# First FFN feature blocks in pieces of 384 and 128 tokens instead of 256 and 256, with another order of all instructions

## The chip, the cores and the metric

The kernel runs on one core of a Trainium2 chip. The metric is the device time of one execution in microseconds (us), lower is better. The median of several runs is given, and beside it one profiled execution, from which all views of the trace come. The engines are TensorE (PE, its weight loads shown apart as PEld), VectorE (DVE), ScalarE (ACT) and GpSimd (POOL); SyncE (SP) issues the transfers.

## The reference

One layer of a hybrid backbone: 512 latent tokens that are also given 256 context tokens, width 1024. Three token mixers (gated linear attention, an S5 state space, grouped-query attention) read one input projection and are merged by gates. What the change touches is the FFN behind them, of 2816 gated features with a convolution of width 3 over the tokens:

```python
def dwconv3(x, w, b):
    xp = jnp.pad(x, ((0, 0), (1, 1), (0, 0)))
    return xp[:, :-2] * w[0] + xp[:, 1:-1] * w[1] + xp[:, 2:] * w[2] + b

def conv_ffn(h, lp):
    u = dwconv3(h @ lp["ffn_up"], lp["ffn_conv_w"], lp["ffn_conv_b"])
    a, v = jnp.split(u, 2, axis=-1)
    return (jax.nn.silu(a) * v) @ lp["ffn_down"]
...
        m_lat = jnp.split((jax.nn.silu(c) @ ada_w[i] + ada_b[i])[:, None, :], 6, axis=-1)
        h_lat = modulate(rms_norm(x, norm_mix_pre[i]), m_lat[0], m_lat[1])
        y_ctx, y_lat = token_mixer(h_ctx, h_lat, lp, rope, not last)
        x = x + m_lat[2] * rms_norm(y_lat, norm_mix_post[i])
        h_lat = modulate(rms_norm(x, norm_ffn_pre[i]), m_lat[3], m_lat[4])
        x = x + m_lat[5] * rms_norm(conv_ffn(h_lat, lp), norm_ffn_post[i])
```

## The kernel before

Each large product is made of three matmuls in fp32r (`mm3`): every operand is split into a high and a low half, and high x high, low x high and high x low are summed in PSUM. So `wuph` and `wupl` are the high and low half of a block of up weights `wup`, `h2h` and `h2l` those of the normalised FFN input. A matmul holds a 128x128 tile of weights, which it loads itself (a PEld record), and streams the tokens through as columns.

The FFN runs over 22 feature blocks of 128 (`NF`), each with two parts, `up{i}0` for the gate and `up{i}1` for the value. A part loads its weights (D), makes the high copy and the low difference, sums 8 slices of the width in one PSUM bank of 512 tokens, and ends with an affine on ScalarE and two convolution steps on VectorE. For blocks 2 to 21 a part has 24 matmuls of 512 columns. For the first two blocks (`NHALF = 2`) the tokens are taken in two pieces, so that each of four parts has 48 matmuls: the first piece can begin before the last tokens are ready. Tokens come ready 128 at a time: `res{t}` adds the mixer's result to the residual for token tile t = 0 to 3, and `h2{t}{n}` scales one half of the width into `tmp`, transposes it with four matmuls into `h2T`, modulates it into `y`, and splits that into `h2h` and `h2l`. The matmuls of the mixer's output projection and of the down projection `ffn_down` write tiles named `tk`, the gate projections `bg`, and the S5 state space has `pT`, `Z`, `win`, `x`, `y5`.

Nothing is ordered by the order of the code. Every instruction is recorded first, and a table `PLACE` gives for each part a letter for each of its instructions (P TensorE, V VectorE, A ScalarE, G GpSimd, D transfer) and a rank; each engine then issues its instructions by rank, and tile buffers are allotted in that order. All instructions are issued by one helper, so the profile has one line, L1223, for nearly all of them, and groups are told apart by tile names.

The loop of the up projection before the change:

```python
            nh = 2 if i < NHALF else 1
            w_ = TL // nh
            for hf in range(nh):
                sl = slice(hf * w_, hf * w_ + w_)
                for k in range(KT):
                    mm3(b[:, sl], wh[:, k * P:k * P + P], wl[:, k * P:k * P + P], h2h[k][:, sl], h2l[k][:, sl],
                        k == 0 and hf == 0, k == KT - 1 and hf == nh - 1, skip_group_check=True)
```

Of the kernel before, what the change touches and what calls it, by code (L numbers as in the profile page):

```python
# [2662 lines left out]
```

## Time and profile before

| | |
|---|---|
| median of 3 runs | 912.75 us (912.71 to 914.13) |
| profiled execution | 912.98 us |
| its span | 910.8 us |
| TensorE busy | 876.1 us, 96% of the span, 4800 matmuls |
| VectorE busy | 612.6 us, 67%, 1118 instructions |
| ScalarE busy | 372.2 us, 41%, 728 |
| GpSimd busy | 230.7 us, 25%, 155 |

The span is what the profile shows; the device time has some 2 us around it. A busy share is an average over stages: the mixer runs to about 531 us, the FFN from there to the end, and each has to be read by itself.

### The profile page before, as it was taken

Reading aid. Unit: us, or ns where it says so; the run is one execution under the profiler, and the core shown is the slowest. Engines: PE = TensorE matmul, PEld = TensorE weight load, DVE = VectorE, ACT = ScalarE, POOL = GpSimd, SP = SyncE. Lnnn points to the kernel's source line nnn. Section 1 sums busy time; section 2 is a strip of 40 time slices with the busy share of each in tenths; the row PEclk is TensorE's granted clock in tenths of the full one; section 3 lists DMA queues with packets and bytes.
Section 4 is the critical chain, followed back from the end, with each engine's and each line's share of the span. In section 5 each row is a group of like instructions: output and inputs, shape, how many; then the busy total and the mean of one; then the engine's idle time right before and its main releaser. Section 6 shows DMA issues by size and latency. Waiting matters only on the chain. (4 is left out here: it accounts for less than half of the span.)

```text
span 910.8 us, 12672 instructions
## 1 busy us (share of the span) xinstructions
PE 876.1 (96%) x4800; PEld 710.8 (78%) x4800; DVE 612.6 (67%) x1118; ACT 372.2 (41%) x728; POOL 230.7 (25%) x155
## 2 busy tenths in 40 slices
PE   6999999989999999999999989999999999999996
PEld 5587867666678888887787868988888888878885
DVE  6988699898985434388967793554556657964223
ACT  3455457567686522044643472233222223420111
POOL 1032002223532333655264133201111023052200
PEclk9999999999999999999999989999999999999999
DMA  9922352230312221437767002221332333432201
GB/s 349 402 81 70 105 150 98 80 133 1 125 47 70 70 93 47 173 108 289 267 220 242 1 1 93 93 93 53 109 116 93 107 103 108 169 116 93 69 24 70
DMA packets 39644, 107.69 MB, mean 118 GB/s; under 512 B 7214, under 2 KB 10942, under 8 KB 39584
## 3 DMA queue, kind: packets, MB, share of 16 engines
q1 hardware_dynamic: 39584, 106.88, 34.1%
q8 instruction: 38, 0.62, 0.3%
q14 instruction: 22, 0.18, 0.1%
HBM read 103.49 MB, written 3.38 MB: 117 GB/s over the span
## 5 line engine op out<-in xcount | busy, mean ns | idle before, releaser
L1223 PE MATMUL up<-h2h,wuph 128*128 128x512 f32 (+1 forms) x384 | 134.4, 374 | 0.5 <-DVE h2h L1223 0.3
L1223 PE MATMUL up<-h2l,wuph 128*128 128x512 f32 (+1 forms) x384 | 134.1, 373 | 0.0
L1223 PE MATMUL up<-h2h,wupl 128*128 128x512 f32 (+1 forms) x384 | 133.6, 372 | 0.0
L1223 DVE SCALAR_TENSOR_TENSOR u<-up,col,u 128x511 f32<-128x511 f32 x88 | 64.6, 746 | 41.0 <-ACT u L1223 39.9
L1223 POOL TENSOR_TENSOR wupl<-wup,wuph 128x1024 fp32r<-128x1024 f32 x15 | 36.9, 2463 | 184.4 <-PE up L1223 93.0
L1223 PEld LDWEIGHTS up<-h2h,wuph 128*128 128x128 f32 x384 | 71.8, 189 | 14.2 <-DVE h2h L1223 0.7
L1223 ACT ACTIVATE u<-up,col 128x512 f32<-128x512 f32 x44 | 33.9, 778 | 118.9 <-PE up L1223 115.0
L1223 PEld LDWEIGHTS up<-h2l,wuph 128*128 128x128 f32 x384 | 72.2, 188 | 13.0
L1223 PEld LDWEIGHTS up<-h2h,wupl 128*128 128x128 f32 x384 | 71.7, 188 | 12.7
L1223 PE MATMUL bg<-hh,wbgl 128*128 128x512 f32 x192 | 75.5, 399 | 1.1 <-DVE wbgl L1223 0.9
L1223 PE MATMUL bg<-hl,wbgh 128*128 128x512 f32 x192 | 75.6, 399 | 0.0
L1223 PE MATMUL bg<-hh,wbgh 128*128 128x512 f32 x192 | 75.2, 398 | 0.0
L1223 DVE TENSOR_TENSOR wupl<-wup,wuph 128x1024 fp32r<-128x1024 f32 x29 | 36.1, 1246 | 45.7 <-PE up L1223 31.1
L1223 PE MATMUL tk<-wtkh,gl 128*128 128x512 f32 x176 | 64.5, 390 | 0.7 <-DVE gl L1223 0.7
L1223 PE MATMUL tk<-wtkh,gh 128*128 128x512 f32 x176 | 64.7, 389 | 0.0
L1223 PE MATMUL tk<-wtkl,gh 128*128 128x512 f32 x176 | 64.6, 389 | 0.0
L1223 POOL TENSOR_TENSOR j<-ada,cbc 128x1024 f32<-128x1024 f32 x16 | 39.9, 2494 | 37.3 <-ACT jb L1223 8.1
L1223 PEld LDWEIGHTS bg<-hh,wbgl 128*128 128x128 f32 x192 | 36.1, 188 | 11.0 <-DVE wbgl L1223 2.0
L1223 PEld LDWEIGHTS bg<-hl,wbgh 128*128 128x128 f32 x192 | 36.1, 188 | 8.9 <-issue 2.0
L1223 PEld LDWEIGHTS bg<-hh,wbgh 128*128 128x128 f32 x192 | 35.9, 188 | 7.7 <-issue 1.0
L1223 PEld LDWEIGHTS tk<-wtkh,gl 128*128 128x128 f32 x176 | 33.0, 188 | 7.9 <-DVE gl L1223 1.1
L1223 POOL TENSOR_TENSOR wbgl<-wbg,wbgh 128x1024 fp32r<-128x1024 f32 x6 | 18.5, 3084 | 81.2 <-DVE wbgh L1223 45.0
(491 smaller groups left out, 2045.9 us busy)
## 6 DMA issues: line engine op xcount, KB each, us to landing
ada<-in_ada SPq DMA_DIRECT2D x48, 512.0 KB
wup<-in_wup SPq DMA_DIRECT2D x44, 512.0 KB
wbg<-in_wbg SPq DMA_DIRECT2D x24, 512.0 KB
wtk<-in_wdn SPq DMA_DIRECT2D x22, 512.0 KB
wP<-in_wP SPq DMA_DIRECT2D x16, 512.0 KB
wbr<-in_wbr SPq DMA_DIRECT2D x8, 512.0 KB
wo<-in_wout SPq DMA_DIRECT2D x16, 256.0 KB
w<-in_wB SPq DMA_DIRECT2D x8, 384.0 KB
```

What stands on the lines that cost most here:

```text
L1223: r = getattr(self.real[e], m)(*a, **k)
```

## The change

The token pieces of the first two feature blocks become 384 and 128 instead of 256 and 256 columns. The number of matmuls stays, 48 for each of four parts; 96 have 384 columns and 96 have 128.

```diff
-            nh = 2 if i < NHALF else 1
-            w_ = TL // nh
+            parts_ = ((0, 3 * P), (3 * P, TL)) if i < NHALF else ((0, TL),)
+            nh = len(parts_)
             for hf in range(nh):
-                sl = slice(hf * w_, hf * w_ + w_)
+                sl = slice(*parts_[hf])
...
-    "up201": ("DAGPPPPPPPPPPPPPPPPPPPPPPPPAVV",
+    "up201": ("DVGPPPPPPPPPPPPPPPPPPPPPPPPAVV",
...
```

The table `PLACE` has new ranks for nearly every instruction, and some letters change: VectorE has as many letters as before (1102), ScalarE 609 instead of 614, GpSimd 156 instead of 151. Of the low halves `wupl`, GpSimd makes 19 instead of 15 and VectorE 25 instead of 29. The following rows show the order at three places.

First, TensorE's queue at the entry to the FFN, before the change. `h2T_1120` and `h2T_1123` are the transposes of token tile 2, `h2T_1134` and `h2T_1137` those of tile 3, `up_1147` is a part of the first blocks, `up_1246` and `up_1356` are whole blocks:

```order
L1223 MATMUL h2T_1120_1193<-cst_1_68,tmp_1119_1192 128x128 x3
L1223 MATMUL up_1147_1220<-h2h_1075_1148,wuph_1145_1218 128x256
L1223 MATMUL h2T_1120_1193<-cst_1_68,tmp_1119_1192 128x128
L1223 MATMUL up_1147_1220<-h2l_1079_1152,wuph_1145_1218 128x256
L1223 MATMUL h2T_1123_1196<-cst_1_68,tmp_1122_1195 128x128 x4
L1223 MATMUL h2T_1134_1207<-cst_1_68,tmp_1133_1206 128x128 x4
L1223 MATMUL h2T_1137_1210<-cst_1_68,tmp_1136_1209 128x128 x4
L1223 MATMUL up_1246_1319<-h2h_1075_1148,wuph_1244_1317 128x512
L1223 MATMUL up_1356_1429<-h2h_1075_1148,wuph_1354_1427 128x512
```

And at the same place after the change:

```order
L1223 MATMUL h2T_1120_1193<-cst_1_68,tmp_1119_1192 128x128 x4
L1223 MATMUL h2T_1123_1196<-cst_1_68,tmp_1122_1195 128x128 x4
L1223 MATMUL h2T_1109_1182<-cst_1_68,tmp_1108_1181 128x128
L1223 MATMUL h2T_1134_1207<-cst_1_68,tmp_1133_1206 128x128 x4
L1223 MATMUL up_1147_1220<-h2h_1075_1148,wuph_1145_1218 128x384
L1223 MATMUL up_1147_1220<-h2l_1079_1152,wuph_1145_1218 128x384
L1223 MATMUL h2T_1137_1210<-cst_1_68,tmp_1136_1209 128x128 x4
L1223 MATMUL up_1246_1319<-h2h_1075_1148,wuph_1244_1317 128x512
L1223 MATMUL up_1356_1429<-h2h_1075_1148,wuph_1354_1427 128x512
```

The two first matmuls of `up_1147` are 384 columns wide and stand behind the transposes of `h2T_1134`, no longer among those of `h2T_1120`; the whole blocks follow at the same row.

Second, TensorE's queue where the second piece of the part `up_1142` begins, after the change (before it, the same part has 256-column rows):

```order
L1223 MATMUL up_1142_1215<-h2h_1078_1151,wupl_1141_1214 128x384
L1223 MATMUL up_1142_1215<-h2h_1078_1151,wuph_1140_1213 128x384
L1223 MATMUL up_1142_1215<-h2l_1082_1155,wuph_1140_1213 128x384
L1223 MATMUL up_1142_1215<-h2h_1078_1151,wupl_1141_1214 128x384
L1223 MATMUL up_1142_1215<-h2h_1075_1148,wuph_1140_1213 128x128
L1223 MATMUL up_1142_1215<-h2l_1079_1152,wuph_1140_1213 128x128
L1223 MATMUL up_1142_1215<-h2h_1075_1148,wupl_1141_1214 128x128
L1223 MATMUL up_1142_1215<-h2h_1075_1148,wuph_1140_1213 128x128
L1223 MATMUL up_1142_1215<-h2l_1079_1152,wuph_1140_1213 128x128
```

From the fifth of these rows on the 128-column matmuls of one part stand one behind another: all 24 lie within 28 rows.

Third, TensorE's queue in the S5 stretch, before the change. `bg` are gate matmuls, `y5_340` reads the states `x__334` and `x__337`:

```order
L1223 MATMUL bg_624_696<-hh_103_170,wbgl_623_695 128x512
L1223 MATMUL bg_624_696<-hh_109_176,wbgh_622_694 128x512
L1223 MATMUL bg_624_696<-hl_110_177,wbgh_622_694 128x512
L1223 MATMUL uT_358_430<-cst_1_68,ug1_357_429 128x96 x2
L1223 MATMUL y5_340_412<-r1_306_378,x__334_406 64x128 x4
L1223 MATMUL y5_340_412<-i1_308_380,x__337_409 64x128 x2
L1223 MATMUL bg_624_696<-hh_109_176,wbgl_623_695 128x512
L1223 MATMUL y5_340_412<-i1_308_380,x__337_409 64x128 x2
```

After the change:

```order
L1223 MATMUL bg_624_696<-hh_98_165,wbgh_622_694 128x512
L1223 MATMUL y5_340_412<-r1_306_378,x__334_406 64x128 x4
L1223 MATMUL bg_624_696<-hl_99_166,wbgh_622_694 128x512
L1223 MATMUL bg_624_696<-hh_98_165,wbgl_623_695 128x512
L1223 MATMUL bg_624_696<-hh_103_170,wbgh_622_694 128x512
L1223 MATMUL bg_624_696<-hl_104_171,wbgh_622_694 128x512
L1223 MATMUL bg_624_696<-hh_103_170,wbgl_623_695 128x512
L1223 MATMUL bg_624_696<-hh_109_176,wbgh_622_694 128x512
L1223 MATMUL y5_340_412<-i1_308_380,x__337_409 64x128 x4
```

Six `bg` matmuls now stand between the two halves of `y5_340`, where none stood. Over the stretch from the last `Z_326` to the first `win_353` there are 63 `bg` matmuls in place of 55.

## Rows read from the trace of the kernel before

**Rows 1.** The page: engine totals, and the chain that ended last by line

```profile
PE 876.1 (96%) x4800; PEld 710.8 (78%) x4800; DVE 612.6 (67%) x1118; ACT 372.2 (41%) x728; POOL 230.7 (25%) x155
...
PE up L1223 26%; PE tk L1223 16%; DMA wup<-in_wup 0%; DVE tmp L1223 0%; PE h2T L1223 0%; DVE ml L1223 0%; POOL wtkl L1223 0%; DVE gl L1223 0%; DVE y L1223 0%; DVE wtkl L1223 0%; DVE wupl L1223 0%; DVE rsy L1223 0%; ACT wuph L1223 0%; DVE rsx L1223 0%; DVE x L1223 0%
```

**Rows 2.** Windows of 20 us at the entry to the FFN and in it

```profile
core 0: us, PE busy (x) PEld busy (x) DVE busy (x) ACT busy (x) POOL busy (x), PEclk, DMA share, GB/s
520.00:540.00 20.00, 16.32 (x81) 13.62 (x80) 17.91 (x69) 15.94 (x49) 2.68 (x4) 0.88 0.00 1
540.00:560.00 20.00, 19.70 (x108) 16.89 (x107) 10.05 (x23) 6.75 (x15) 10.55 (x9) 0.95 0.22 77
560.00:580.00 20.00, 20.00 (x112) 17.47 (x111) 7.24 (x9) 5.01 (x6) 4.91 (x3) 1.00 0.17 56
800.00:820.00 20.00, 19.27 (x86) 15.63 (x85) 15.35 (x15) 6.83 (x9) 12.61 (x8) 1.00 0.38 132
```

**Rows 3.** TensorE's groups, `up`: shape, count, busy us, mean ns, idle us before

```profile
L1223 PE MATMUL up<-h2h,wuph 128*128 128x512 f32 x320 | 117.6, 392 | 0.5 <-DVE h2h L1223 0.3 <-ACT wuph L1223 0.2
L1223 PE MATMUL up<-h2h,wupl 128*128 128x512 f32 x320 | 117.3, 390 | 0.0
...
L1223 PE MATMUL up<-h2h,wuph 128*128 128x256 f32 x64 | 18.4, 287 | 0.0
```

**Rows 4.** Timeline (start us, length us, ...): first and last of 18 gate matmuls

```profile
192.26 0.39 PE L1223 MATMUL bg<-hl,wbgh 128*128 128x512 f32 x1
...
196.13 0.39 PE L1223 MATMUL bg<-hh,wbgh 128*128 128x512 f32 x1
```

**Rows 5.** Timeline of TensorE, first and last of 17 matmuls of 256 columns

```profile
555.00 0.28 PE L1223 MATMUL up<-h2h,wuph 128*128 128x256 f32 x1
...
556.92 0.28 PE L1223 MATMUL up<-h2l,wuph 128*128 128x256 f32 x1
```

**Rows 6.** Weight loads by line and shape, with 128, 32 and 8 columns

```profile
L1223 PEld LDWEIGHTS up<-h2h,wupl 128*128 128x128 f32 x384 | 71.7, 188 | 12.7
...
L1223 PEld LDWEIGHTS ada<-ada,cpad 128*32 128x32 f32 x128 | 3.6, 112 | 4.1 <-issue 1.2 <-DVE cpad L1223 1.0 <-DMA cT<-in_cT 0.4
...
L1223 PEld LDWEIGHTS row<-cst,acc 128*8 128x8 f32 x2 | 0.2, 86 | 0.0
```

**Rows 7.** Timeline, four matmuls of 2 columns and their loads

```profile
21.06 0.52 PEld L1223 LDWEIGHTS ada<-cst,adar 128*128 128x128 f32 x4 [1.50 <-ACT adar L1223]
21.06 0.61 PE L1223 MATMUL ada<-cst,adar 128*128 128x2 f32 x4 [1.02 <-ACT adar L1223]
```

**Rows 8.** Waits of TensorE: total us, times, longest

```profile
PE h2T L1223 <- DVE tmp L1223: 3.7, 1, 3.7
...
PE y L1223 <- DVE x__337_409 L1223: 1.4, 1, 1.4
```

**Rows 9.** Timeline of TensorE at the entry to the FFN

```profile
536.08 0.90 PE L1223 MATMUL h2T<-cst,tmp 128*128 128x128 f32 x3 [3.68 <-DVE tmp L1223]
536.88 0.58 PE L1223 MATMUL up<-h2h,wuph 128*128 128x256 f32 x1
...
537.43 0.55 PE L1223 MATMUL up<-h2l,wuph 128*128 128x256 f32 x1
```

**Rows 10.** Windows of the S5 stretch, a later one, and one in the entry

```profile
170.00:180.00 10.00, 8.46 (x46) 6.70 (x44) 9.91 (x17) 2.86 (x5) 0.00 (x0) 1.00 0.10 26
180.00:190.00 10.00, 6.32 (x57) 3.84 (x59) 9.89 (x14) 7.06 (x21) 5.91 (x2) 1.00 0.00 0
240.00:260.00 20.00, 18.05 (x122) 13.16 (x121) 19.26 (x52) 16.32 (x47) 11.48 (x15) 1.00 0.08 30
...
536.00:537.00 1.00, 0.92 (x4) 0.62 (x4) 1.00 (x6) 1.00 (x4) 0.00 (x0) 0.50 0.03 8
```

**Rows 11.** Groups by line: `wupl` on GpSimd and on VectorE

```profile
L1223 POOL TENSOR_TENSOR wupl<-wup,wuph 128x1024 fp32r<-128x1024 f32 x15 | 36.9, 2463 | 184.4 <-PE up L1223 93.0 <-ACT wuph L1223 26.5 <-DVE u L1223 23.9
...
L1223 DVE TENSOR_TENSOR wupl<-wup,wuph 128x1024 fp32r<-128x1024 f32 x29 | 36.1, 1246 | 45.7 <-PE up L1223 31.1 <-ACT wuph L1223 9.6 <-POOL wupl L1223 4.2
```

More of the change, by code (lines that the diff above doesn't have):

```diff
@@ L285 @@
+        1717, 1720, 1721, 1724]),
+    "rope2": ("VVVVVVAVPPPPVAVAVPPPPA",
+        [1109, 1519, 1672, 1665, 1677, 1680, 1682, 1688, 1711, 1713, 1714, 1722, 1727, 1709, 1715, 1687, 1700, 1723,
+        1725, 1726, 1729, 1733]),
+    "rope3": ("VVVVVVAVPPPPVAVAVPPPPV",
+        [970, 1432, 1603, 1611, 1623, 1633, 1636, 1649, 1654, 1655, 1656, 1658, 1735, 1638, 1652, 1641, 1663, 1659,
+        1660, 1661, 1667, 1738]),
     "ropec0": ("VGAVAVPPPPAA",
-        [1110, 1545, 1564, 1584, 1568, 1588, 1570, 1592, 1607, 1608, 1612, 1621]),
+        [1107, 1353, 1563, 1581, 1571, 1588, 1573, 1583, 1585, 1593, 1598, 1605]),
@@ L303 @@
-    "ap010": ("AAVVGVPPPPAAAVVVGPPPPAPPPPA",
-        [2033, 2043, 2053, 2055, 2060, 2071, 2074, 2076, 2077, 2087, 2095, 2026, 2056, 2073, 2080, 2084, 2093, 2091,
-        2092, 2094, 2096, 2105, 2089, 2090, 2103, 2106, 2111]),
+        [1894, 1900, 1891, 1892, 1977, 1980, 1893, 1896, 1908, 1932, 1992, 2019, 2021]),
+    "ap010": ("AAVVGVPPPPAAAVVGGPPPPAPPPPA",
+        [2030, 2042, 2052, 2055, 2062, 2058, 2069, 2070, 2085, 2088, 2091, 2025, 2053, 2066, 2067, 2071, 2079, 2093,
+        2094, 2097, 2099, 2103, 2089, 2090, 2101, 2105, 2110]),
@@ L306 @@
     "at011": ("PPPPPPPPVVVVV",
[L307 to L310 removed]
+        [1898, 1913, 1866, 1871, 1889, 1915, 1880, 1881, 1916, 1926, 1936, 1942, 1945]),
+    "ap011": ("AAVVGGPPPPAAAVVVGPPPPAPPPPV",
+        [1949, 1955, 1963, 1976, 1985, 1993, 2040, 2041, 2043, 2044, 2048, 1959, 1967, 1984, 1997, 2008, 2013, 2033,
+        2034, 2036, 2038, 2064, 2014, 2016, 2018, 2023, 2028]),
@@ L323 @@
+    "ap101": ("AAVVGGPPPPAAAVVGGPPPPVPPPPV",
+        [1878, 1884, 1895, 1901, 1927, 2118, 2132, 2134, 2136, 2138, 2142, 1899, 1888, 1944, 1947, 1953, 1951, 2122,
+        2124, 2126, 2127, 2151, 2140, 2141, 2143, 2144, 2155]),
     "pv10": ("PPPPPPPPPPPP",
-        [2165, 2166, 2169, 2170, 2172, 2174, 2175, 2177, 2180, 2181, 2184, 2185]),
+        [2166, 2167, 2170, 2171, 2173, 2174, 2178, 2179, 2182, 2183, 2186, 2187]),
     "at110": ("PPPPPPPPVVVVV",
-        [2029, 2030, 1984, 1987, 2023, 2025, 2007, 2008, 2013, 2036, 2044, 2054, 2057]),
@@ L327 @@
-    "ap110": ("AAVVVGPPPPAAAVVGGPPPPAPPPPA",
-        [2067, 2062, 2075, 2078, 2088, 2099, 2098, 2101, 2104, 2110, 2117, 2086, 2081, 2097, 2100, 2107, 2115, 2119,
-        2121, 2123, 2124, 2127, 2108, 2112, 2125, 2128, 2134]),
+        [2027, 2029, 1981, 1983, 2020, 2024, 2006, 2007, 2012, 2037, 2045, 2054, 2056]),
+    "ap110": ("AAVVGGPPPPAAAVVGGPPPPAPPPPA",
+        [2068, 2059, 2077, 2080, 2087, 2095, 2100, 2104, 2107, 2108, 2115, 2083, 2076, 2092, 2096, 2102, 2112, 2113,
+        2114, 2117, 2119, 2123, 2109, 2111, 2120, 2121, 2130]),
@@ L362 @@
-    "bg05": ("DAVPPPPPPPPPPPPPPPPPPPPPPPPA",
-        [1913, 2140, 2198, 2304, 2307, 2308, 2309, 2310, 2313, 2314, 2330, 2331, 2334, 2335, 2337, 2338, 2341, 2342,
-        2343, 2345, 2348, 2349, 2350, 2351, 2353, 2354, 2357, 2359]),
-    "br05": ("PPPPPPVV",
-        [2192, 2199, 2257, 2401, 2403, 2404, 2406, 2412]),
+        [1553, 1706, 1719, 2231, 2234, 2236, 2305, 2312, 2324, 2326, 2331]),
+    "bg05": ("DVVPPPPPPPPPPPPPPPPPPPPPPPPA",
+        [1923, 2139, 2197, 2298, 2301, 2302, 2304, 2306, 2308, 2309, 2310, 2313, 2314, 2315, 2316, 2317, 2318, 2319,
+        2320, 2321, 2333, 2336, 2337, 2339, 2341, 2344, 2345, 2351]),
@@ L367 @@
+    "br05": ("PPPPPPVG",
+        [2191, 2199, 2256, 2399, 2400, 2402, 2404, 2410]),
     "bg06": ("DVGPPPPPPPPPPPPPPPPPPPPPPPPA",
-        [1128, 1311, 1322, 1371, 1373, 1375, 1391, 1392, 1394, 1397, 1398, 1399, 1400, 1401, 1403, 1404, 1406, 1407,
-        1408, 1409, 1410, 1412, 1414, 1435, 1447, 1451, 1455, 1601]),
+        [1134, 1305, 1315, 1314, 1387, 1391, 1395, 1399, 1401, 1403, 1404, 1405, 1408, 1409, 1410, 1412, 1424, 1426,
+        1428, 1430, 1433, 1435, 1446, 1450, 1451, 1454, 1456, 1566]),
@@ L375 @@
     "br07": ("PPPPPPVG",
-        [2444, 2447, 2448, 2450, 2451, 2452, 2456, 2468]),
+        [2443, 2446, 2448, 2449, 2450, 2451, 2455, 2468]),
     "gw": ("DAVV",
-        [1908, 1974, 2129, 2136]),
+        [1911, 1982, 2125, 2131]),
     "gz0": ("PAVA",
-        [2252, 2254, 2267, 2289]),
+        [2252, 2254, 2265, 2269]),
     "gz1": ("PAVA",
-        [2407, 2409, 2425, 2414]),
+        [2403, 2406, 2425, 2411]),
     "gz2": ("PAVA",
-        [2325, 2332, 2364, 2344]),
+        [2330, 2342, 2357, 2347]),
@@ L493 @@
+    "tp30": ("DAVDAVDVGDVGPPPPPPPPPPPPPPPPPPPPPPPPAVV",
+        [2630, 2666, 2747, 2633, 2687, 2738, 2797, 2836, 2842, 2820, 2866, 2904, 2858, 2860, 2864, 2867, 2869, 2871,
+        2872, 2873, 2874, 2875, 2880, 2884, 2885, 2886, 2888, 2895, 2900, 2903, 2941, 2954, 2956, 2959, 2969, 2973,
+        2975, 3019, 3097]),
     "tp31": ("PPPPPPPPPPPPPPPPPPPPPPPPAVG",
-        [2787, 2789, 2790, 2792, 2794, 2869, 2883, 2884, 2885, 2891, 2892, 2893, 2895, 2896, 2898, 2901, 2902, 2903,
-        2904, 2963, 2966, 2971, 2974, 2975, 3018, 3058, 3088]),
+        [2809, 2811, 2812, 2813, 2814, 2865, 2879, 2882, 2883, 2887, 2889, 2892, 2894, 2896, 2897, 2898, 2899, 2901,
+        2902, 2952, 2961, 2964, 2966, 2971, 3023, 3059, 3081]),
@@ L501 @@
-        2911, 2949, 2950, 2955, 2958, 3003, 3013, 3096, 3110]),
+        [2764, 2768, 2770, 2771, 2773, 2774, 2777, 2778, 2781, 2782, 2783, 2787, 2854, 2856, 2868, 2876, 2877, 2878,
+        2911, 2947, 2948, 2951, 2963, 2993, 3012, 3087, 3131]),
     "sso": ("VAVVVVV",
-        [3418, 3430, 3433, 3435, 3437, 3439, 3442]),
+        [3423, 3433, 3437, 3440, 3443, 3445, 3447]),
     "og0": ("VVVVPPPPA",
-        [3537, 3525, 3539, 3490, 3575, 3577, 3578, 3579, 3582]),
+        [3550, 3537, 3539, 3503, 3575, 3576, 3578, 3579, 3582]),
```

167 lines of the change are left out of this document (73 added, 94 removed), and 974 rows, old and new, of the table PLACE.

## The prediction

> **What bounds the kernel now.** I read the page's totals and its chain first. TensorE is busy 876.1 of 910.8 us, and the chain that ended last runs through `up` and `tk` matmuls, 26% and 16% of the span, with almost nothing else in it [rows 1]. A total says nothing of a single stage, so the table of 20 us windows came next. The reader should compare two of its columns, TensorE's busy time and the granted clock: from 560 on TensorE is busy the whole 20 us at clock 1.00, and even the window at 800, the poorest I read there, has 19.27 [rows 2]. What is added to TensorE in the FFN therefore arrives at the end almost one for one. The exception is the entry to the FFN, 520 to 560, with 16.32 and 19.70 of 20 and a clock of 0.88 and 0.95 [rows 2]. The changed pieces are issued from there on, in the first 45 us or so of the FFN.
>
> The profiled execution took 912.98 us, its span is 910.8, so 2.2 us lie around the span. The median of the three runs is 912.75, 0.2 us lower; the sum goes by 912.98. Within 0.2% is within 1.8 us, about what a measurement of this kernel can tell from no change.
>
> **Term 1: the pieces.** Four parts (`up00`, `up01`, `up10`, `up11`) change their 48 matmuls each: 192 of 256 columns leave, 96 of 384 and 96 of 128 come. The same columns pass, so the price hangs on what a matmul costs beyond its columns. The grouped rows give 390 to 392 ns for 512 columns and 287 for 256 [rows 3], but those are durations of overlapping instructions. The pace is the distance between starts: for 512 columns, over a run of 18 gate matmuls, (196.13 - 192.26)/17 = 227.6 ns [rows 4]; for 256, over 17 in a row, (556.92 - 555.00)/16 = 120 ns [rows 5]. Two points make a line: (227.6 - 120)/256 = 0.42 ns a column, and 227.6 - 512 x 0.42 = 12.4 ns that every matmul costs. A 384-column piece is inside it: 173.8 ns.
>
> A 128-column piece is outside it. By the line it is 66.2 ns, and a pair 66.2 + 173.8 = 240, the same as two of 256: a price of nothing. But each piece also loads its own 128x128 weights, and the load's own pace may be slower than 66.2 ns. Loads overlap matmuls, and each other, since a record of 188 ns repeats every 120 ns [rows 5, 6]; their floor is below 120 ns and unseen there. Two views bound it. First the load's duration against the columns loaded: 188 ns for 128, 112 for 32, 86 for 8 [rows 6]; (188 - 86)/120 = 0.85 ns a column at most, (188 - 112)/96 = 0.79 at least, so the part that grows is 101 to 109 ns, some 105. Second, a place where a matmul has next to no columns: four matmuls of 2 columns, each with its 128x128 load. Their loads are on record for 0.52 us, so (0.52 - 0.19)/3 = 110 ns from one to the next, and the matmuls for 0.61, (0.61 - 0.25)/3 = 120 [rows 7]. With 2 columns nothing but the load can set that pace. The three values, 105, 110 and 120, average to 112 ns, which I take: a matmul cannot follow another faster than its weights, so a 128-column piece costs 112, not 66.2.
>
> A pair then costs 112 + 173.8 - 240 = 45.8 ns more, times 96 = **+4.4 us**. The load that a 256-column piece hides (112 under 120) is no longer covered by 128 columns: that is the whole mechanism. Bounds: with the load hidden 0; at 105 ns a load (105 + 173.8 - 240) x 96 = +3.7; at 120, +5.2. Above 120 it can't be by the load, since 256-column pieces with the same load run at 120. Two bounds from farther rows: if the 12.4 ns were no part of a short piece, -1.2, and if a 128-column piece cost what a 512 one does (227.6), (227.6 + 173.8 - 240) x 96 = +15.5. I stay near the load's rows, which have the same load; the extremes have neither its shape nor its reason.
>
> The Trainium skill ("TensorE: Matmul & The Clock Gate", section "LDWEIGHTS (loading the stationary operand)") has a load take its columns divided by 1.2 ns, 107 ns for 128, which speaks against short pieces. The growth in the trace, 0.79 to 0.85 ns a column, agrees [rows 6]. By that figure the term would be (107 + 173.8 - 240) x 96 = +3.9.
>
> **Term 2: the entry to the FFN.** TensorE stands 3.68 us at 532.40 for a `tmp` from VectorE, the largest wait there is [rows 8, 9]. The order after has the same transposes before that wait and the same `tmp` scalings, additions and splits on VectorE ahead, so I find nothing that shortens it. What moves is small: the two first matmuls of `up_1147` stood between transposes of token 2 as 256-column pieces, and stand after them, as 384, in the changed order. In the rows they take 0.58 and 0.55 us each at the lower clock (0.50 granted, 1.2 GHz of 2.4) against 0.28 at full clock [rows 5, 9, 10], so 128 more columns there cost 128 x 0.42 x 2 = 0.11 us each, 0.2 in all, if they are not waiting for the last token's `tmp` anyway, which they mostly are. Nothing queues behind them but the last four transposes. I put the term at **0**, bounds -1 (a third of the wait filled) to +1.
>
> **Term 3: the other order.** The S5 stretch is where the order shows most. Between 170 and 190 TensorE has 8.46 and 6.32 of 10 us, VectorE 9.91 and 9.89 [rows 10]: VectorE paces it, TensorE waits. The changed order puts 63 gate matmuls `bg` (of 512 columns) between the last `Z_326` and the first `win_353` where 55 stood, six of them in the middle of `y5_340`, where TensorE now waits 1.4 us for `x__337_409` [rows 8]. Eight matmuls of 227 ns are 1.8 us of work that would fill a hole and be missing later. But later VectorE is still near full (19.26 of 20 from 240 to 260) [rows 10], so what TensorE gains is partly waited for again; I credit about a quarter of 1.8, a choice: **-0.5**. Against it stand four more `wupl` subtractions on POOL (15 to 19), at 2.46 us each where VectorE takes 1.25 [rows 11], hidden while a weight block is loaded blocks ahead; uncovered they cost 1.2 us each, 4.9 in all. Copies and subtractions of the first 30 us that moved between VectorE and ScalarE I cost at nothing: input transfers cover them. So bounds are -1.8 to +4.9.
>
> **Sum:** 912.98 + 4.4 + 0 - 0.5 = **916.9 us**.
>
> **Rivals.**
> Load hidden: the 128-column pieces keep their line, or nearly, since each load is done while earlier pieces still stream. For it: records of loads overlap [rows 6]. Against: within a run of `up_1142` 24 short pieces stand within 28 rows of the order, so a backlog of loads has nothing to hide under. It gives 912.98 + 0 - 0.5 = 912.5, the same. The Trainium skill's section "Back-to-back issue gap" on the same page has 81 ns as sustained spacing at 128 columns, so (81 + 173.8 - 240) x 96 = +1.4 and 913.9, the same too; its 131 ns at 512 columns is far from the 227 here [rows 4], so I trust it little.
>
> The S5 holes are filled, the side of faster: the six `bg` take the whole 1.4 us wait for `x__337_409`, the two others a little more, and all 1.8 us are kept to the end. For it: the six stand exactly there. Against: VectorE at 9.9 of 10. With the pieces at nothing it gives 911.2, with the pieces at their lower bound of -1.2 it gives 910.0; I take the middle, 910.6. It decides only where the pieces cost nothing or less; at my price for them it ends at 915.6, slower.
>
> The order costs: three of the four `wupl` moved to POOL come late and hold their block 1.2 us each. For it: POOL's 2.46 us; against: in two of the three kinds of 512-column `up` matmul, the low half of the weights among them, all waits come to 0.5 us [rows 3]. It gives 916.9 + 3.6 = 920.5.
>
> Short pieces priced like long ones: 912.98 + 15.5 - 0.5 = 928.0. For it only the rows where duration falls less than columns do; the pace [rows 4, 5] speaks against.
>
> **How the numbers follow.** Forecast 0.53, its own range 914.8 to 918.8 (bounds of +3.7 to +5.2 for the pieces and -1.8 to +1 for the rest). Load hidden 0.18, S5 filled 0.16, the order costs 0.10, priced like long 0.03. Faster 0.16, same 0.18, slower 0.53 + 0.10 + 0.03 = 0.66. The range goes from 911.5, which takes in most of the hidden case, to 920.5, which takes in the dearer order: left out are the faster case and the 928.0, 0.19.
>
> **What would show it.** Right: in the changed profile the starts of 128-column matmuls lie 105 to 120 ns apart and those of 384 about 174; load records back to back in those runs; the wait for `tmp` still 3.7 us; the windows from 560 on at 20 of 20, and the last `tk` ends 3 to 5 us later. Wrong: 66 ns between short starts (hidden), or a stage ahead of 530 that ended microseconds earlier or later, which would make term 3, not the pieces, the story. What I could not price is an order re-made on all engines: its sum of many small waits is the likeliest cause of a miss.

## The result, and the profile after

The changed kernel took 925.16 us as a median of 4 runs (922.18 to 929.87), the kernel before 913.44 beside it (912.71 to 917.14): a ratio of 1.0123, with a 95% interval of 1.0094 to 1.0152. Measured again later (run 9) it gave 1.0158 (1.0143 to 1.0172). It is slower, as forecast, but by 11.7 us where 3.9 were forecast, and outside the range of 911.5 to 920.5. The mean granted clock of TensorE differs from run to run, for the kernel before too (0.984 to 0.991 over all its runs here), and the longer runs are by and large those with the lower mean; the spread of both kernels cannot be understood without that.

The profiled execution took 925.87 us, its span is 924.0, some 13 us over that of before. The page's totals and its chain by line:

```profile
PE 886.7 (96%) x4800; PEld 720.2 (78%) x4800; DVE 606.6 (66%) x1118; ACT 370.6 (40%) x723; POOL 237.1 (26%) x160
...
PE up L1223 26%; PE tk L1223 17%; PE bg L1223 14%; PE tp L1223 11%; PE br L1223 4%; PE b1a L1223 2%; PE oatt L1223 1%; PE bo L1223 1%; PE ada L1223 1%; PE Z L1223 1%; PE b1c L1223 1%; DVE i L1223 1%; PE pt L1223 1%; PE win L1223 1%; PE suf L1223 1%
```

The gain in TensorE's busy time, 10.6 us, looks like added matmul work. It isn't all of that kind: at half clock the same matmul is busy for longer (0.63 us instead of 0.39 in the rows at 88 us below). The windows tell it apart (columns as in [rows 2]):

```profile
80.00:100.00 20.00, 17.61 (x73) 14.17 (x72) 15.25 (x26) 7.73 (x20) 4.67 (x4) 0.91 0.23 66
87.72:91.13 3.41, 3.22 (x8) 2.54 (x9) 3.41 (x8) 0.81 (x2) 0.79 (x2) 0.50 0.00 1
...
180.00:190.00 10.00, 7.00 (x43) 4.28 (x41) 9.89 (x16) 6.81 (x17) 2.06 (x1) 1.00 0.37 127
190.12:196.94 6.82, 5.84 (x31) 3.24 (x33) 6.23 (x11) 2.90 (x8) 0.38 (x1) 0.50 0.00 0
400.00:420.00 20.00, 18.99 (x225) 16.53 (x224) 17.05 (x34) 6.24 (x12) 11.56 (x8) 0.91 0.25 85
520.00:540.00 20.00, 20.00 (x90) 16.57 (x89) 14.53 (x50) 11.66 (x32) 0.00 (x0) 1.00 0.04 13
540.00:560.00 20.00, 16.41 (x78) 13.69 (x77) 17.55 (x60) 15.28 (x42) 4.67 (x6) 0.83 0.00 2
560.00:580.00 20.00, 20.00 (x107) 17.61 (x106) 6.99 (x9) 5.96 (x7) 9.58 (x4) 1.00 0.30 106
800.00:820.00 20.00, 20.00 (x90) 16.56 (x89) 13.31 (x16) 5.43 (x7) 5.56 (x3) 1.00 0.26 93
```

The column to read is the granted clock, the third from the end. Before, it was under 1.00 only in the first 40 us, at the entry to the FFN and at the end. Now it is 0.91 in the windows at 80 and at 400, and between 180 and 200 a stretch from 190.12 to 196.94 has 0.50, which is 1.2 GHz of 2.4. The entry lies 10 us later, at 541 to 551, and from there on TensorE is as full as before, or fuller: the window at 800 has 20.00 where it had 19.27 [rows 2], and no window of 20 us from 560 to 900 is under 19.95.

The pieces, by grouped rows (answer to [rows 3]) and by the timeline of a run of 128-column matmuls:

```profile
L1223 PE MATMUL up<-h2h,wupl 128*128 128x512 f32 x320 | 118.4, 390 | 0.0
...
L1223 PE MATMUL up<-h2h,wuph 128*128 128x384 f32 x32 | 11.0, 348 | 0.0
...
L1223 PE MATMUL up<-h2h,wuph 128*128 128x128 f32 x32 | 8.5, 265 | 0.0
```

```profile
566.82 0.22 PE L1223 MATMUL up<-h2h,wuph 128*128 128x128 f32 x1
566.88 0.27 PE L1223 MATMUL up<-h2l,wuph 128*128 128x128 f32 x1
566.99 0.27 PE L1223 MATMUL up<-h2h,wupl 128*128 128x128 f32 x1
...
568.11 0.28 PE L1223 MATMUL up<-h2h,wuph 128*128 128x128 f32 x1
```

From 566.88 to 568.11 there are 11 steps, (568.11 - 566.88)/11 = 112 ns; the median of all adjacent starts is 111, and 174 for 384 columns. The first short one starts 0.17 behind a 384-column one, the second only 0.06 behind the first. TensorE's waits after (answer to [rows 8]; more of them here), and behind them four of before:

```profile
PE h2T L1223 <- DVE tmp L1223: 3.6, 1, 3.6
...
PE tp L1223 <- DVE hcl L1223: 2.4, 1, 2.4
PE pT L1223 <- DVE i L1223: 2.3, 1, 2.3
...
PE tr L1223 <- DVE kd L1223: 1.9, 2, 1.5
...
PE Z L1223 <- DVE pT L1223: 1.9, 2, 1.3
...
PE y L1223 <- DVE x__334_406 L1223: 1.1, 1, 1.1
...
PE ba L1223 <- DVE so L1223: 1.0, 1, 1.0
...
PE y L1223 <- DVE x__337_409 L1223: 0.2, 1, 0.2
```

```profile
PE pT L1223 <- DVE r L1223: 2.5, 1, 2.5
PE tp L1223 <- DVE hcl L1223: 2.2, 1, 2.2
...
PE tr L1223 <- DVE kd L1223: 0.2, 1, 0.2
PE Z L1223 <- ACT pT L1223: 0.2, 1, 0.2
```

The wait for `tmp` stayed (3.6 where it was 3.7), that for `x__337` shrank from 1.4 to 0.2 as the six `bg` filled it, and a wait of 1.1 for `x__334` came ahead of it: VectorE, busy for 9.89 of the 10 us from 180 on, stayed the bound there, and the hole moved. Elsewhere in the mixer three waits are new or longer: for `kd` (1.9 instead of 0.2), for `pT` (1.9 instead of 0.2) and for `so` (1.0, none before). `hcl` and `i` are waits of 2.4 and 2.3, of a size that before had as well (2.2 for `hcl`, 2.5 for `r`). What differs is what follows them, here for `hcl`:

```profile
85.13 0.39 PE L1223 MATMUL tp<-wPl,hc 128*128 128x512 f32 x1
87.91 0.79 PE L1223 MATMUL tp<-wPh,hcl 128*128 128x512 f32 x1 [2.39 <-DVE hcl L1223]
88.50 0.63 PE L1223 MATMUL tp<-wPh,hc 128*128 128x512 f32 x1
...
90.64 0.63 PE L1223 MATMUL tp<-wPl,hc 128*128 128x512 f32 x1
```

The wait for `hcl` ends at 87.91, and the matmuls behind it start (90.64 - 88.50)/5 = 428 ns apart instead of 227: the clock fell at 87.72 and rose at 91.13, for 8 matmuls 1.6 us. In the profile of before the same matmul waited nearly as long, and its window is undisturbed (first row below). Run 9, the changed kernel once more, has the same wait as the profile above, and the matmuls behind it keep their pace (the other rows):

```profile
80.00:100.00 20.00, 17.81 (x79) 14.44 (x78) 15.73 (x30) 9.07 (x21) 6.08 (x5) 1.00 0.33 93
```

```profile
89.38 0.50 PE L1223 MATMUL tp<-wPh,hcl 128*128 128x512 f32 x1 [2.38 <-DVE hcl L1223]
89.72 0.39 PE L1223 MATMUL tp<-wPh,hc 128*128 128x512 f32 x1
...
90.87 0.39 PE L1223 MATMUL tp<-wPl,hc 128*128 128x512 f32 x1
```

There the five steps are (90.87 - 89.72)/5 = 230 ns each.

At the entry, transposes and the two 384-column pieces ran at half clock, as the 256-column ones did [rows 9]:

```profile
546.35 3.13 PE L1223 MATMUL h2T<-cst,tmp 128*128 128x128 f32 x13 [3.59 <-DVE tmp L1223]
549.13 0.67 PE L1223 MATMUL up<-h2h,wuph 128*128 128x384 f32 x1
549.62 0.69 PE L1223 MATMUL up<-h2l,wuph 128*128 128x384 f32 x1
```

And `wupl` on GpSimd, 19 in place of 15 [rows 11], held up no `up` matmul: all nine groups of `up`, three of them above, show 0.0 us of idle time ahead.

```profile
L1223 POOL TENSOR_TENSOR wupl<-wup,wuph 128x1024 fp32r<-128x1024 f32 x19 | 45.7, 2410 | 182.3 <-PE up L1223 70.9 <-DVE wuph L1223 46.5 <-DVE wupl L1223 35.2
```

### The profile page after: what moved, and what is told of

It reads as the page before. It is cut to its first block, busy times and chain, and to the rows that moved or that the text cites. A ratio compares the mean times of both kernels' runs of the same rounds, so it can differ in the third digit from the quotient of the medians.

```text
span 924.0 us, 12694 instructions
## 1 busy us (share of the span) xinstructions
PE 886.7 (96%) x4800; PEld 720.2 (78%) x4800; DVE 606.6 (66%) x1118; ACT 370.6 (40%) x723; POOL 237.1 (26%) x160
## 4 chain that ended last, share of the span: by engine, by line
PE 85%; DVE 9%; ACT 2%; issue 2%; DMA 1%; POOL 0%; SPq 0%; DVEq 0%; ACTq 0%
PE up L1223 26%; PE tk L1223 17%; PE bg L1223 14%; PE tp L1223 11%; PE br L1223 4%; PE b1a L1223 2%; PE oatt L1223 1%; PE bo L1223 1%; PE ada L1223 1%; PE Z L1223 1%; PE b1c L1223 1%; DVE i L1223 1%; PE pt L1223 1%; PE win L1223 1%; PE suf L1223 1%
## 5 line engine op out<-in xcount | busy, mean ns | idle before, releaser
L1223 PE MATMUL up<-h2l,wuph 128*128 128x512 f32 (+2 forms) x384 | 136.9, 376 | 0.0
L1223 PE MATMUL up<-h2h,wuph 128*128 128x512 f32 (+2 forms) x384 | 136.7, 378 | 0.0
L1223 PE MATMUL up<-h2h,wupl 128*128 128x512 f32 (+2 forms) x384 | 135.9, 376 | 0.0
L1223 POOL TENSOR_TENSOR wupl<-wup,wuph 128x1024 fp32r<-128x1024 f32 x19 | 45.7, 2410 | 182.3 <-PE up L1223 70.9
L1223 DVE TENSOR_TENSOR wupl<-wup,wuph 128x1024 fp32r<-128x1024 f32 x25 | 30.6, 1223 | 34.0 <-PE up L1223 30.3
L1223 ACT CAST wuph<-wup 128x1024 fp32r<-128x1024 f32 x25 | 26.0, 1050 | 40.7 <-PE up L1223 29.9
L1223 PEld LDWEIGHTS tk<-wtkl,gh 128*128 128x128 f32 x176 | 33.0, 188 | 7.3 <-DVE wtkl L1223 0.5
```

What stands on the lines that cost most here:

```text
L1223: r = getattr(self.real[e], m)(*a, **k)
```

## Where the time went, stage by stage

For this the starts of two instructions were read from every trace: the last transpose at the entry, and the last matmul of all. Up to the first is the mixer with the entry, from it to the second the FFN. The FFN runs at full clock but for its first 1 to 3 us, into which the half clock at the entry reaches in the runs without fillers (1.8 us before, 1.2 after). The third column adds up the time ahead of the entry, without the stretch at the entry itself, in which the granted clock was 0.50. Each row is one execution.

```
                                    last transpose  to last matmul  at 0.50 before entry
before                                  540.1 us        363.3 us          6.8 us
after                                   550.7           365.8            23.9
after, again                (run 9)     548.1           365.9            17.1
after, pieces 256/256       (run 1)     550.8           361.7            23.9
after, filled waits         (run 5)     550.8           365.6            23.9
after, filled, 256/256      (run 18)    544.9           361.9            10.2
before, 128/384             (run 2)     541.3           368.3            17.1
before, 64/448              (run 3)     543.4           371.6            20.5
mixer before, FFN after     (run 4)     541.9           365.9            13.7
the same, 256/256           (run 10)    541.7           362.2            10.2
before, filled              (run 6)     541.7           362.7            17.1
before, filled, 128/384     (run 12)    541.6           367.3            13.7
```

So of the 13.1 us between the two profiled executions, 10.6 arise ahead of the FFN and 2.5 in it.

What a stretch at half clock costs can be read from the two executions of the changed kernel (after and run 9), since the same matmul can be compared in both. Starts in us, and behind each place the time at 0.50 there:

```
                                     after     run 9   difference   at 0.50 there, after and run 9
ahead of the wait for hcl            85.13     86.61     -1.48
behind it                            92.04     92.01     +0.03       3.4 and 0 us
end of the wait for i               191.10    191.05     +0.05
behind it                           198.23    197.12     +1.11       6.8 and 3.4
behind the wait for so              411.53    410.44     +1.09
5 us on                             417.07    414.43     +2.64       3.4 and 0
last transpose of the entry         550.74    548.07     +2.67
```

The difference grows at these three places, by 1.5, 1.1 and 1.6 us, each time for 3.4 us more at half clock, and between them it stays within 0.1. So 10.2 us more at half clock cost 4.1 in the same code, 0.40 for each.

The mixer from its first matmul that reads `hcl` to the first transpose of the entry took 450.3 us before (80.2 to 530.5), 458.2 after (82.6 to 540.9) and 454.1 in run 9, with 0, 13.7 and 3.4 us at 0.50 in it. TensorE's waits of over 150 ns in it add up to 13.0, 16.0 and 16.0 us.

## Experiments: the pieces

**Run 1, the changed order with pieces of 256.**

```diff
-            parts_ = ((0, 3 * P), (3 * P, TL)) if i < NHALF else ((0, TL),)
+            parts_ = ((0, 256), (256, TL)) if i < NHALF else ((0, TL),)
```

> The changed order, with pieces of 256 and 256 as before. Theory A (a matmul cannot follow another faster than its weights, so a 128-column piece costs 111 ns and the pieces cost 96 x 45 ns): 4.4 us less than the changed kernel, so about 920.5, and 7 us over the kernel before remain as the price of the order. Rival B (the pieces cost nothing, the whole loss is the order): no less than the changed kernel, about 925. Rival C (the pieces also spoil the entry to the FFN, so all of the loss is theirs): 913.

Measured 921.54 us (917.81 to 923.6), 1.0071 (1.0049 to 1.0093) of before. It is 3.6 under the changed kernel by the medians and 4.4 by the lowest runs, and in the table the FFN gets shorter by 365.8 - 361.7 = 4.1 with the entry at the same place. Theory A; 7.9 us by the medians and 5.1 by the lowest runs stay over the kernel before, with nothing of the pieces left in them.

**Runs 2 and 3, the order of before with 128/384 and with 64/448**, the same line with `(0, 128), (128, TL)` and `(0, 64), (64, TL)` in the kernel before.

> The order of before, with pieces of 128 and 384 tokens in this sequence. Theory A: the same 96 short and 96 long pieces, so +4.4 us, about 917.5, with starts of 128-column matmuls 111 ns apart. Rival B (short pieces hide their load): no change, 913. Rival C (most of the 11.7 us is the pieces): 920 or more.

> The order of before, with pieces of 64 and 448 tokens. Theory A: the load's pace is a floor, so a 64-column piece costs the same 111 ns as one of 128, and the pair 111 + 201 - 240 = 72 ns more than two of 256, times 96 = +6.9 us, about 920. Rival B (cost by columns, 12 ns a matmul beside them): 39 + 201 = 240, no change, 913. Rival D (a short piece costs in proportion above its columns, so 64 costs 50 ns less than 128): about +2, 915.

Run 2: 921.34 (917.99 to 922.65), 1.0069 (1.0048 to 1.0090). Run 3: 923.11 (920.11 to 924.67), 1.0089 (1.0066 to 1.0111). By the medians run 2 lost 7.7, over theory A's 4.4 and the number of rival C (920 or more), and run 3 lost 9.5 where 6.9 were expected; by the lowest runs (5.3 and 7.4) and by the FFN's stretch (+5.0 and +8.3) theory A is the nearest. The floor itself shows in the timeline of run 3, first and last of six 64-column matmuls:

```profile
554.48 0.28 PE L1221 MATMUL up<-h2h,wuph 128*128 128x64 f32 x1
...
555.04 0.28 PE L1221 MATMUL up<-h2h,wupl 128*128 128x64 f32 x1
```

(555.04 - 554.48)/5 = 112 ns for 64 columns, where by columns it would be 39: rival B and rival D are out. In run 2's profile the entry comes 1.2 us later than before, with 17.1 us at 0.50 ahead of it against 6.8; that the rest of its median is the clock too is not shown, but run 12 speaks for it.

**Run 12, the order of before with 128/384 and filled waits** (fillers below).

> The order of before with fillers and with pieces of 128 and 384: against the kernel before with fillers (913.3, runs 912.9 to 914.2) only the pieces differ, and the clock doesn't. Theory A: 96 x 45 ns = +4.4 us, 917.7, runs close together. Rival G (the pieces cost more than their matmuls, the +7.7 us of the run without fillers being theirs): 921.

918.91 (917.9 to 920.92), 1.0060 (1.0047 to 1.0073) of before: 5.6 by the medians over run 6, whose code differs in the pieces alone, though it was measured beside other runs of before (915.45 and 915.06). The profiles have 4.6 in the FFN's stretch, with the entry at the same place (541.6 and 541.7). Rival G's 921 lies above all its runs, and the price of run 2's pieces was not 7.7.

**Run 9, the changed kernel again**, unedited, beside runs 10 to 12.

> The changed kernel once more, beside the three that follow. Theory A (pieces +4.4, a slower mixer +7 at equal clock, less 2 us of FFN waits that are gone, and up to some us by the granted clock, which differs from run to run): lowest runs 9 us over the lowest of before, the median 10 to 12 over its median. If theory B holds (chance of the chip that was used): under 6 us.

928.06 (923.37 to 929.03), 1.0158 of before: 11.2 over the lowest of before where 9 were expected, 13.0 by the medians where 10 to 12 were. Theory B's 6 is out.

## Experiments: the order, by stages

**Run 4, the mixer's numbers of before with the FFN of after; run 10, the same with 256/256.** The table `PLACE` is put together from both: parts `up`, `th`, `mm22` and `out` from the change, all others from before.

> Numbers of before for all parts of the mixer, up to the transposes at the entry, and the changed numbers and the 384 and 128 pieces for the FFN. Theory A with the order's loss in the mixer (half-clock stretches behind waits, a slower start): +4.4 for the pieces, less about 2.5 us of FFN waits that the changed order lacks, so +2, about 915, with the granted clock low only in the first 30 us, at the entry and at the end. Rival E (the loss of the order sits in the FFN or in its early loads and casts): 920 or more.

> The mixer's numbers of before, the FFN's numbers of the change, pieces of 256 and 256: the run with 384 and 128 had its lowest at 915.2, 2.4 over before. Theory A (pieces 4.4): 4.4 us below that run, lowest about 910.8, 2 us faster than before, since the FFN's waits of 0.4, 0.9 and some smaller ones are gone. Rival B (the pieces cost less in this order): 913 to 915.

Run 4: 919.5 (915.15 to 920.65), 1.0046 (1.0030 to 1.0062); by the medians that is 5.9 over before, nearer to rival E's 920 than to the 915 expected; the profile has the clock low only where it was expected. Run 10: 913.11 (911.31 to 915.88), 0.9992 (0.9979 to 1.0006). The lowest runs are 2.4 over and 0.9 under those of before, where 2 over and 2 under were expected; the FFN's stretch has 3.7 us for the pieces. For the FFN's order it has 361.7 - 363.3 = -1.6 (run 1 against before), -1.1 (run 10 against before), and with fillers -0.8 and -0.4 (runs 18 and 11 against run 6). The FFN part of the change without its pieces is a small gain, too small to be told by run 10's times; so with the mixer of before the loss of the order is gone (run 10 against run 1), and it lies in the mixer's order.

## Experiments: the waits and the clock

**Run 5, the changed kernel with fillers; run 6, the kernel before with fillers.** A filler is a matmul with a weight tile of zeros into a sum that is under way, or a transpose of the identity into a tile that the next transposes overwrite; it stands in TensorE's order right ahead of the instruction that waits.

```diff
+        if sc.part_ == "tp05" and first:
+            fill("fill1", 10, lambda: PE.matmul(acc, lhsT=zr, rhs=bh, start=False, stop=False, **kw))
...
+            if q == 3 and src is pi4:
+                fill("fill2", 20, lambda: PE.transpose(b[:, 0:P], ident, ident))
...
+            if t == 2 and n == 0:
+                fill("fill3", 32, lambda: PE.transpose(b[:, 0:P], ident, ident))
```

> The changed kernel with work of no effect put into three of TensorE's waits: 10 matmuls with a zero weight tile before the wait for hcl (2.4 us), 20 transposes of the identity before the one for i (2.3 us), 32 before the one for tmp at the entry (3.6 us). The waits stay, only TensorE is busy in them. Theory A (of the order's loss, the part behind those waits is the granted clock of 0.50 that follows each of them): the half-clock stretches at 88, 190 and 545 us go, worth 3.4/2 us for the first and about as much for each of the others, where VectorE paces too: about 5 us less than the changed kernel, 920. Rival B (the low clock costs nothing where VectorE paces, or doesn't depend on what TensorE does in the wait): 925, or more by fillers that reach past the wait.

> The kernel before with the same fillers, 10 before the wait for hcl, 20 before the one for r in the S5 stretch, 32 before the one for tmp. Theory A: the half-clock stretch of 6.8 us at the entry (535 us) goes, and with it up to 2 us, and the runs with a mean clock of 0.985 join those with 0.990: about 911. Rival B (VectorE sets the pace of the entry, TensorE's clock there is hidden): 913, no change.

Run 5: 923.94 (922.81 to 925.64), against 925.16 and 928.06 for the changed kernel: 1.2 to 4.1 less, where 5 were expected, and no lower at its lowest (922.81 against 922.18): between theory A and rival B. Its windows:

```profile
20.00:40.00 20.00, 17.45 (x138) 9.10 (x127) 16.85 (x54) 5.44 (x10) 0.39 (x2) 0.78 1.03 403
80.00:100.00 20.00, 19.88 (x94) 16.25 (x93) 16.55 (x30) 9.59 (x23) 4.71 (x4) 1.00 0.26 83
180.00:200.00 20.00, 18.19 (x132) 12.73 (x131) 19.13 (x31) 13.10 (x33) 2.60 (x1) 1.00 0.26 94
400.00:420.00 20.00, 18.99 (x212) 16.38 (x211) 15.55 (x29) 5.27 (x10) 11.41 (x8) 0.83 0.19 65
540.00:560.00 20.00, 18.39 (x112) 15.30 (x111) 17.86 (x62) 15.76 (x43) 4.69 (x6) 1.00 0.01 2
```

The three stretches are gone: 1.00 at 80, 180 and 540. But this execution had more of the low clock at the start (0.78 where the changed kernel's profile has 0.83) and 6.8 us of it in the window at 400, around the wait of 1.0 for `so`, which has no filler. So the entry came no earlier.

Run 6: 913.32 (912.87 to 915.91), against 915.45 for before (911.99 to 917.65), 0.9989 (0.9975 to 1.0002). Its lowest is no lower, but 11 of 12 runs lie below 914.3, where 9 of the 17 of before lie above 915.4. The entry with fillers:

```profile
520.00:540.00 20.00, 19.55 (x113) 16.51 (x112) 17.61 (x71) 15.38 (x48) 1.03 (x2) 1.00 0.01 2
540.00:560.00 20.00, 18.98 (x110) 16.12 (x109) 12.07 (x28) 7.81 (x18) 10.62 (x11) 1.00 0.16 54
```

```profile
534.56 3.66 PE L1232 MATMUL h2T<-cst 128*128 128x128 f32 x32
538.41 0.55 PE L1232 MATMUL h2T<-cst,tmp 128*128 128x128 f32 x3 [0.19 <-DVE tmp L1232]
...
540.74 1.27 PE L1232 MATMUL h2T<-cst,tmp 128*128 128x128 f32 x8 [0.25 <-ACT tmp L1232]
542.79 0.50 PE L1232 MATMUL up<-h2h,wuph 128*128 128x512 f32 x1 [0.77 <-DVE h2h L1232]
```

The clock is 1.00, the wait for `tmp` is filled from 534.56 on, and yet the transposes that follow wait again, 0.25 for `tmp` from ScalarE and then 0.77 for `h2h`. So VectorE and ScalarE set most of the entry's pace, as rival B has it, but not all of its low clock was hidden: from the first transpose behind the wait for `tmp` to the last matmul of all it is 367.3 us before and 366.0 in run 6, and 366.6 and 365.7 in runs 10 and 11, which also differ in the fillers alone. That is about 1 us for the low clock at the entry, where theory A had up to 2. In the profiled execution it is used up by 10.3 us more at 0.50 ahead of the entry, and the ratio of run 6 does not clear 1; 911 was not reached.

**Run 18, the changed order with fillers and 256/256; run 17, the changed mixer with the FFN of before and fillers.**

> The whole changed order with fillers and with pieces of 256 and 256; against the changed kernel with fillers (923.9, with 384 and 128) only the pieces differ. Theory A: 4.4 to 5.6 us less, about 919. Rival G (in the changed order the pieces cost more, since their 128-column runs stand one behind another): under 917.

> The whole mixer's numbers of the change, the FFN's of before, pieces of 256 and 256, fillers in the waits for hcl, i and tmp. Against the kernel before with fillers (913.3) only the mixer's order differs, at nearly the same granted clock. Theory W (the sum of the changed kernel: pieces 4.4 to 5.6, FFN order -2, so of its 10.6 with fillers the mixer's order is about +7): about 920. Rival V (most of it is made up in the second half): 916 or less.

Run 18: 917.07 (913.87 to 921.98), 1.0036 (1.0018 to 1.0054). That is 6.9 under run 5 by the medians, 2 us below theory A's 919 and at the edge of rival G's 917. The two profiled executions are 9.6 apart, and the table parts them: 365.6 - 361.9 = 3.7 in the FFN's stretch, as for the pieces elsewhere, and 5.9 ahead of it, 550.8 against 544.9, in a mixer whose code is the same. Run 18's windows show where:

```profile
20.00:40.00 20.00, 16.07 (x147) 8.71 (x140) 17.32 (x58) 5.43 (x10) 0.39 (x2) 0.91 1.03 404
80.00:100.00 20.00, 19.88 (x91) 16.18 (x91) 16.37 (x28) 9.15 (x23) 5.09 (x5) 1.00 0.22 66
180.00:200.00 20.00, 18.18 (x131) 12.81 (x130) 19.74 (x34) 14.95 (x35) 2.61 (x1) 1.00 0.17 61
400.00:420.00 20.00, 18.99 (x251) 16.45 (x249) 18.27 (x36) 5.26 (x17) 10.96 (x9) 1.00 0.23 73
```

0.91 against 0.78 at 20, 1.00 against 0.83 at 400. Matmul by matmul, run 5 is 1.8 us behind run 18 at 60 us, where the waits for the input transfers differ as well, 2.0 at 405, 5.1 at 417, and 5.2 from there to the transposes of the entry: 6.8 us at half clock cost 3.2 there, 0.46 for each. The last 0.8 of the 5.9 arise among the entry's transposes, where the pieces stand, so they belong to the pieces: counted from the first 512-column `up` matmul, these cost 4.4 here. Fillers also tell how much of the order's loss hangs on the clock: with pieces of 256 the changed order is 7.9 over before without them (run 1) and 3.3 with them (run 18), with pieces of 384 and 128 it is 11.7 to 13.0 and 8.5 (run 5), by the medians; the ratios are 1.0071 and 1.0036, and 1.0123 to 1.0158 and 1.0102, and some of their intervals overlap. Run 17: 920.59 (919.44 to 923.25), 1.0066 (1.0050 to 1.0083), theory W's 920 by its number, but with 30.7 us at 0.50 and the entry at 551.2, so it shows the clock as much as the order.

**Run 11, the best of it together**: mixer of before, FFN order of the change, 256/256, fillers.

> The same with fillers in the waits for hcl, r and tmp. Theory A (fillers change no pace at full clock, but keep the runs from the lower clock): lowest as the run without them, about 911, and the spread of 3 us gone, so the median about 911 too, against 913 without. Rival (fillers do nothing): the same median and spread as without.

912.71 (912.14 to 913.77) against 915.06 for before (912.22 to 916.8): 0.9989 (0.9979 to 0.9998). The spread is gone, as expected, but the lowest and the median are 912.1 and 912.7 where 911 was expected; it is the only version here that is faster than both kernels beyond its interval, by 0.1%.

## Experiments: which part of the mixer's order

**Runs 7 and 8, the changed kernel with the start, or the S5 parts and their gate matmuls, of before. Runs 13 to 16, the filled kernel before with the start, the S5 parts, the attention parts of the change, and with all three.** In each, the rows of `PLACE` of the named parts were exchanged.

> The changed kernel with the numbers of before for the first 45 us: loads, modulation, the two normalisations, the first products. The trace of the changed kernel has lost 2.4 us against before by the time that 50 us of matmuls are done. Theory A (the start's loss is its own and reaches the end): 2 to 2.5 us less than the changed kernel, about 922.5. Rival E (VectorE-paced S5 stretch takes the gain back): 925.

> The changed kernel with the numbers of before for the S5 parts and the gate matmuls bg that fill them. Theory A: the S5 stretch and what lies behind it (from 100 to 220 us) lost about 5 us more than before, of which 3.4 us by the clock after the wait for i; with the order of before there some 3 to 5 us less than the changed kernel, about 921. Rival F (the loss lies with the attention and gated-linear-attention parts between them, not with S5): 925.

> The kernel before with fillers in three waits (913.3), and the changed numbers for the start alone (loads, modulation, normalisations, first products). Theory S (the changed start is 2.4 us later, as its trace shows at 50 us, and the VectorE-paced part behind it keeps that): about 915.5. Theory T (start and S5 stretch are each harmless, the loss comes from their meeting): 913.

> The same with the changed numbers for the S5 parts and the gate matmuls bg2 and br2 alone. Theory S (the S5 stretch of the change loses some 4 us by itself): about 917. Theory T: 913. Theory of the record's third term (eight more bg matmuls fill a hole): 912.

> The same with the changed numbers for attention, rotary and first token products alone. Theory S (the loss is in start and S5): 913 to 914. Rival U (VectorE's order in the attention parts is what holds the S5 chain up): 916 or more.

> The same with all three together: the changed order up to 275 us, that of before behind it, pieces of 256. The trace of the changed kernel had lost 10 us against before there, some 3 of them by the granted clock behind the waits for hcl and i, which the fillers keep up. Theory S: 913.3 + 6 to 7, about 920. Rival V (what is lost up to 275 us is made up behind it, since TensorE isn't what the second half waits for): under 916.

```
run 7   926.59 us (925.32 to 929.75)   1.0142 (1.0115 to 1.0168)
run 8   926.80    (924.11 to 929.11)   1.0135 (1.0111 to 1.0160)
run 13  916.07    (912.45 to 920.80)   1.0019 (1.0002 to 1.0037)
run 14  921.64    (920.84 to 922.39)   1.0085 (1.0070 to 1.0100)
run 15  922.72    (921.59 to 923.97)   1.0098 (1.0081 to 1.0115)
run 16  917.98    (915.41 to 920.95)   1.0038 (1.0024 to 1.0053)
```

Neither half of the change undone gave anything back (runs 7 and 8). Run 6, with which the others are compared here, was measured beside other runs of before (915.45, and 913.46 for runs 13 to 16). Alone, the S5 parts cost 8.3 us over run 6 by the medians and the attention parts 9.4, and all three together only 4.7 (9.1, 9.9 and 3.7 by the lowest runs against the lowest of before). The start alone costs 2.8 by the medians, as theory S has it, and nothing by the lowest run. The losses do not add up; that would be so if each part's order fits the order that the others had beside it, which is not shown. Theory S and theory T both fail in this form. By exchanging parts the mixer's loss can't be placed.

## Why the prediction was wrong

That the kernel came out slower, as forecast, is owed to the pieces for some 4 of the 12 us only; the rest the forecast had with the other sign.

**Term 1, the pieces: right.** A 128-column piece follows another after 111 ns (112 predicted), a 384-column one after 174 (173.8), and 64 columns cost 112 as well: the pace is set by something that does not shrink with the columns, as the load of 128 columns does not. The sum of +4.4 was measured as +3.7 to +5.0 in the FFN's stretch (runs 1, 2, 4, 12 and 18 against their pairs). Counted from the first 512-column `up` matmul it is 3.9 to 5.0, and 4.4 and 4.6 in the two pairs with fillers, where the clock is 1.00 from the entry on. The rival with the hidden load is out, and with it the 81 ns of the Trainium skill ("TensorE: Matmul & The Clock Gate", section "Back-to-back issue gap"). The Trainium skill, same page, section "LDWEIGHTS (loading the stationary operand)", agrees to 4 ns: columns divided by 1.2 gives an estimate of 107 ns for a load of 128.

**Term 2, the entry: right.** The wait for `tmp` stayed at 3.6, and from the first to the last transpose of the entry it is 9.8 us instead of 9.6.

**Term 3, the other order: the step that failed.** It was put at -0.5, with bounds of -1.8 and +4.9, from the waits of one stretch and from four `wupl`; the start was put at nothing, and the granted clock of the mixer had no term at all. Measured by run 1, which has the other order without the pieces, it is +7.9 us by the medians. What the runs showed in its place, for the two profiled executions: the FFN's order gains 1.6 us (0.4 to 1.6 over the pairs), with waits of 0.2 and 0.7 in the FFN of before gone, and the mixer's loses 10.6, in three parts.

- The start, 2.4 us: the first matmul that reads `hcl` comes at 82.6 instead of 80.2. TensorE's waits up to it are 10.2 instead of 8.9 us, and 10.2 instead of 6.8 us are at 0.50. What of it is order and what is clock is not separated.
- The granted clock behind that, some 5.2 us for 13.7 us at 0.50 where before has none. Of it 4.1 are measured, between two executions of the same kernel (after and run 9); 1.1 for the 3.4 us which run 9 has as well is an estimate, the price of the other 3.4 at that place.
- The order itself, the remaining 2.7 of the 458.2 - 450.3 = 7.9 us. With it goes the growth of TensorE's waits in this stretch from 13.0 to 16.0, the same in run 9: those for `pT`, `kd` and `so` grew by 4.4 in all, and others shrank.

The entry adds 0.2. Runs 6 and 18, with fillers, agree with an order that costs something at any clock: run 18 has its entry 3.2 later, though with 6.9 us less at half clock. The split is rough, since the price of low clock depends on the place: in the mixer of before, 10.3 us more at 0.50, most of them at the start, cost only 1.2 to 1.6 us (runs 2 and 6 against before).

That `wupl` on GpSimd would come late was wrong as a mechanism: `up` waits for nothing. That eight more `bg` would be kept as a gain was wrong too: the hole at `x__337` closed and one at `x__334` opened, as the text had weighed. The prediction did name the sum of many small waits in an order re-made on all engines as the likeliest cause of a miss, and a stage ahead of 530 that ends later as its sign; the entry came 10 us late. Its inner range has a slip on which nothing hangs: by its bounds the upper end is 912.98 + 5.2 + 1 = 919.2, not 918.8.

The error of method was to look for changed waits in one stretch of the mixer, the one from 170 to 190 us, where the three that grew stand outside it (at 165 and 169, 215 and 224, and 411 after), and to price a wait by its length alone. The clock in one trace is a property of the run as well as of the place: the two largest waits of the mixer before, `hcl` and `r`, of 2.2 and 2.5 us, stood in its trace with the clock left at 1.00, and in run 9 so did the one for `hcl`. That a bound was needed for the clock behind each such wait, up to the 1.6 us that the one at 87.91 cost, could be seen from the half-clock rows at the entry.

**Open.** What decides in which execution the clock falls behind a wait of the same length, and why the profiled executions of the changed order show more of it, also with fillers, at the start and at 410 us. Why VectorE brings `pT`, `kd` and `so` later in the changed order, and whether its ranks or its changed engine letters do it: no run separates the two.

## What to carry to other kernels

Short matmuls have a floor, here 111 ns for 128 columns of fp32r with a load of 128 columns each, so that splitting 512 columns as 384 and 128 costs 45 ns more a pair than 256 and 256. Cost a re-ordering by the waits of every stretch, not of the one where the order shows most, and not by the waits alone: add for each long wait of TensorE (2.3 to 3.6 us here, once 1.0) a half-clock stretch that may follow it, and compare the same matmuls in two executions before putting a difference of 1% down to an order. Work of no effect put into such waits is cheap. It narrowed the spread in the order of before (912.1 to 913.8 in run 11), but not in the changed one (913.9 to 922.0 in run 18), and it buys little where another engine sets the pace.
